# Mixer work entered in steps beside weight pieces, in a hybrid encoder layer on one core

## Chip, cores and metric

The kernel runs on one core of one Trainium2 chip. The metric is the device time of one execution in microseconds (us): 1707.37 for the kernel before, the median of 3 runs (1707.24 to 1707.54).

## What is computed

One layer of a bidirectional encoder over 16 learned meta tokens and 256 tokens of width 2048, all in float32. RMSNorm is followed by one input projection that feeds four token mixers and their output gates; then a SwiGLU block and a final RMSNorm:

```
n = rms_norm(h)                        # h: 272 x 2048
p = n @ w_in                           # 14 mixer columns of 512, 4 gates of 2048
z_A = rglru(p)       # conv of width 4, gates, scans both ways, GeLU gate
z_B = hyena(p)       # conv of width 3, long filters from a small sine network, FFT convolution
z_C = retention(p)   # rotary q and k, decay, GroupNorm, swish gate
z_D = hgrn2(p)       # state expansion 128, forget gates, RMSNorm, swish gate
h = h + (sum_b sigmoid(gate_b) * (z_b @ w_branch_out[b])) @ w_out
h = h + (silu(m @ w_gate) * (m @ w_up)) @ w_down      # m = rms_norm(h)
out = rms_norm(h)[16:]
```

## The kernel before

Every large matrix comes from memory in weight **pieces** of 128 x 1024 float32, 568 of them in a fixed order (`piece`, line 97). A piece is loaded into `raw` (4 buffers) by SP's queue, rounded to `hi` by ACT (line 112), and the remainder `lo` = raw - hi is taken by DVE (line 113); `hi` and `lo` have 3 buffers each. The first NPOOL = 2 pieces are split by POOL. The activations are split in the same way, and a product takes three matmuls: hi with hi, hi with low part, lo with hi. `piece` puts its instructions WAHEAD = 250 places ahead in priority; the order on each engine is then made by a scheduler that takes ready instructions by priority, so the order of the program is a priority and no more.

The **head** (lines 196 to 283) loads the meta tokens and x, sums the squares (`squares`), rescales both token tiles (`rescale`; t = 0 and t = 1, in quarters of 512 columns, by ACT and DVE in turn), transposes them on PE (line 280) and writes the split norm `nh`, `nl` (lines 281 and 282).

The **mixer stage** works through SCHED (line 54), a string of 32 letters. A to E are chunks of 256 projected columns for one mixer (`mix_chunk`, 4 pieces, 96 matmuls of 256 to 272 columns, lines 312 to 314); E is the second pair of heads of mixer D; G is a chunk of 512 gate columns for one branch (`gate`, 8 pieces of 12 matmuls of 512 columns, `xs_gemm`). Each mixer is a generator: it yields when it wants its next chunk, and gets the accumulators. What a mixer does after a chunk enters the program there, as one block:

```
            wants[m] = mixers[m].send(mix_chunk(wants[m]))
```

The large blocks are the filters of B (`filters`, line 339, called before B's fourth chunk), B's transforms after its sixth chunk, mixer D's seven levels after its fifth (lines 612 to 637: `ex` and `copy_predicated` into `sc`), C's rotary products and heads (`rotate`, lines 733 to 754), and A's gates and scans (lines 792 to 828), which follow A's second chunk of four. `head_out` (line 484) normalises heads into `on` and transposes them (line 512); `put_z` splits a mixer's result into `zh`, `zl`. Accumulators have 4 buffers, two per chunk; small products share 4 others (`ps`).

After the mixer stage `up` (line 868) multiplies z by the branch weights in the order BORDER = (1, 3, 2, 0), that is B, D, C and A last, 2 pieces each for one quarter of the columns, alternating with the gates of the next quarter. The output projection, SwiGLU and the last norm follow; the change doesn't touch them.

ACT's functions come from tables that are loaded when the set changes; `lut` keeps groups of functions in order. `late` and `add_manual_dep` order an instruction behind another on its engine.

Of the kernel before, what the change touches and what calls it, by code (L numbers as in the profile page):

```python
# [17 lines left out]
P = 128  # L18
D = 2048
# [13 lines left out]
NPOOL = 2  # L33
WPAD = 64
WAHEAD = 250
# [18 lines left out]
SCHED = "BBBBBCDDDDCBCDECEECCGEECCAGAAGAG"  # L54
# [5 lines left out]
for _name, _w in (("norm_mix", 16), ("norm_ffn", 16), ("lcw", 16), ("lcb", 4), ("lba", 8), ("lbx", 8), ("lam", 8),  # L60
                  ("hcw", 36), ("hcb", 12), ("hbias", 4), ("lb", 4), ("b1", 1), ("b2", 1), ("dec", 8),
                  ("negt", 2), ("nyq", 1), ("ind", P), ("fill", 48)):
    PCOL[_name] = _n
    _n += _w
# [3 lines left out]
def body(tc, a, out):  # L68
# [17 lines left out]
    nc.sync.dma_start(par, a["par"])  # L86
# [6 lines left out]

    wpos = [0]
    first = []

    def piece(kt, cols, dst=None, skip=0):

        i = wpos[0]
        wpos[0] += 1  # L100
        with tc.high_priority(offset=WAHEAD if i >= 6 else 0):
# [11 lines left out]
            ins = (G if i < NPOOL else V).tensor_tensor(lo, raw, hi.bitcast(F32), op=SUB)  # L113
# [82 lines left out]
    G.dma_start(mlp, a["mlp"])  # L196
# [12 lines left out]

    def sines():  # L210
        p1 = ps("pf1")
        PE.matmul(p1[:64, :T], mlp[:33, 0:64], mlp[:33, 128:], start=True, stop=True)
        f1 = TT("f1", T, rows=64)
        sine(f1, p1[:64, :T], pc("b1", rows=64))
        p2 = ps("pf2")
        PE.matmul(p2[:64, :T], mlp[:, 64:128], f1, start=True, stop=True)
        sine(f2[:64], p2[:64, :T], pc("b2", rows=64))
        G.memset(f2[64:], 0.0)
# [20 lines left out]
    def squares(g, engs):  # L239
        for q, e in enumerate(engs):  # L240
            dump = H("dump", 512)
            x, acc = quarter(g, q), ss[:, g, q:q + 1]
            if e == "A":
                A.activation(dump, x, AF.Square, accum_out=acc)
            else:
                V.scalar_tensor_tensor(dump, x, 1.0, x, op0=MUL, op1=MUL, accum_out=acc)
        r = rs[:, g:g + 1]
        V.tensor_reduce(r, ss[:, g], op=ADD, axis=mybir.AxisListType.X)
        rsqrt(r, r, 1.0 / D)

    def rescale(g, engs):
        for q, e in enumerate(engs):
            x, r = quarter(g, q), rs[:, g:g + 1]
            if e == "A":
                A.activation(x, x, AF.Copy, scale=r)
            else:
                V.tensor_scalar(x, x, r, None, op0=MUL)
# [18 lines left out]
    split(nh[:, :, 0:META], nl[:, :, 0:META], nm.rearrange("p k b t -> p (k b) t"))  # L276
    for k in range(KT):
        pt = ps("ptn")
        for t in range(2):
# [3 lines left out]
                                         op0=MUL, op1=SUB)]  # L283

# [54 lines left out]
    def filters():  # L339
        sines()  # L340
        late(0, A.activation(adec, par[:, PCOL["dec"]:PCOL["dec"] + 8], AF.Abs))
        w3 = S("w3", 1024)
        G.dma_start(w3, a["hy_w3"])

        dec = S("dec", 1024)
        G.dma_start(dec, a["hy_decay"].partition_broadcast(P))
        A.activation(dec, dec, AF.Abs)
        fwd_t = S("fwd_t", 2, NFREQ)
        G.dma_start(fwd_t, a["dft"])
        split(fwd[0], fwd[1], fwd_t)  # L350
        hs = [H(f"hs{t}", W) for t in range(2)]
        hd = [H(f"hd{t}", W) for t in range(2)]
        hb = [H(f"hb{t}", W) for t in range(2)]
        for t in range(2):
# [10 lines left out]
            V.tensor_tensor(hd[t], e[:, 0:512], hb[t], op=SUB)  # L365
        for s in range(4):
# [11 lines left out]
            A.copy(spec[s % 2][:, s // 2], pk)  # L378

# [11 lines left out]
        V.tensor_tensor(wrap[:, :, 16:31], wrap[:, :, 16:31], ew[:, 4:8, 14::-1], op=SUB)  # L391

    def mixer_b():
# [19 lines left out]
        split(*inv, inv_t)  # L413

# [9 lines left out]
        for t in range(3):  # L424
# [6 lines left out]
            else:  # L431
                A.copy(utm, pu)
                V.tensor_sub(utm[32:64], pu[32:64], utm[32:64].bitcast(F32))
        ys = []
        for f in range(2):
# [18 lines left out]
            if f == 0:  # L454
                G.tensor_copy(y[0][0:1], rr[0:1])
                G.tensor_copy(y[1][0:1], ii[0:1])
            for i in range(2):
                split(yp[0][:, i], yp[1][:, i], y[i])
            ys.append(yp)
        prod = S("prod", NW, META, META)  # L460
# [3 lines left out]
        V.tensor_reduce(ycor, prod, op=ADD, axis=mybir.AxisListType.X)  # L464
        for wp in range(2):
# [14 lines left out]
            put_z(1, 2 * wp, 2, z)  # L480
        yield


    def head_out(b, pos, gate, group, h0=0):
# [4 lines left out]
        if group:  # L489
            mv = tiny("mv", 4 * n, 2)  # L490
            for i in range(4 * n):
                bs = tiny("bs", 6)
                V.bn_stats(bs, pos[i // 4][:, i % 4 * P:i % 4 * P + P])
                V.bn_aggr(mv[:, i], bs)
            rsqrt(rs, mv[:, :, 1], 1.0)
# [6 lines left out]
        for m in range(n):  # L502
# [12 lines left out]
            put_z(b, h0 + 2 * m, 2, z)  # L515

    def silu(dst, src):
        n = dst.shape[-1]
        sg = TT("sg", n)
        A.activation(sg, src, AF.Sigmoid)  # L520
        V.tensor_tensor(dst, src, sg, op=MUL)  # L521

# [3 lines left out]
    def mixer_d(hp):  # L526
# [36 lines left out]
        for c in range(2):  # L563
            silu(gt[:, c], acc[c][:, META:])
# [3 lines left out]
        A.activation(bs.rearrange("p (h c) t -> p h (c t)", h=2), ff[:, :, META:], AF.Ln)  # L568
# [608 lines left out]
```

## Time and profile before

| | |
|---|---|
| median of 3 runs | 1707.37 us |
| the profiled execution's own time | 1708.65 us |
| its span in the trace | 1706.9 us |
| mean granted TensorE clock | 0.996 |
| PE busy | 1667.4 us (98%) |
| DVE busy | 954.6 us (56%) |
| ACT busy | 803.8 us (47%) |
| POOL busy | 80.6 us (5%) |

The profile is of one execution; its times count from the first instruction of the span. PE is TensorE's matmuls, PEld its weight loads, DVE is VectorE, ACT ScalarE, POOL GpSimd, SPq the DMA queue of SyncE. A matmul's end is modelled, so PE counts as busy a little longer than it is. A bracket after a row tells how long the engine stood idle before it and what ended that.

### The profile page before, as it was taken

The page shows a single profiled execution, that of the slowest core. Times are in us where ns is not written, and L with a number is a line of the kernel's source. Part 1 is how long each engine was busy: PE and PEld are TensorE (multiplying, and loading weights), DVE is VectorE, ACT ScalarE, POOL GpSimd, SP SyncE. Part 2 cuts the span into 40 slices and gives each one's busy share as a digit, 9 for nine tenths or more (in the row PEclk, how much of TensorE's full clock was granted, in tenths as well). Part 3 has the DMA queues.
Part 4 walks back from the last instruction along what each step waited for, and adds up shares of the span by engine and source line. Part 5 has one row for each costly group of instructions (what it writes and reads, how often), then busy time and mean ns, then how long its engine had stood idle before and what let it go on. Part 6 is the DMA issues. An engine that isn't in the chain of part 4 may idle for free.

```text
span 1706.9 us, 22379 instructions
## 1 busy us (share of the span) xinstructions
PE 1667.4 (98%) x8844; PEld 1437.0 (84%) x8844; DVE 954.6 (56%) x1140; ACT 803.8 (47%) x969; POOL 80.6 (5%) x74
## 2 busy tenths in 40 slices
PE   6999999999999999999999999999999999999997
PEld 5999999989978888888888888888888888888886
DVE  6755895486675445454455545454545444544554
ACT  5544465474574444444445544444444334444443
POOL 2000000001002002010020000000000000000001
PEclk9999999999999999999999999999999999999999
DMA  6546444546356555555666555555555555555554
GB/s 238 184 140 193 144 140 145 181 139 212 111 172 211 188 194 186 196 194 188 197 198 210 197 197 186 192 190 187 191 190 188 194 196 190 194 185 190 193 191 142
DMA packets 87225, 313.81 MB, mean 184 GB/s; under 512 B 9824, under 2 KB 10112, under 8 KB 86992
## 3 DMA queue, kind: packets, MB, share of 16 engines
q1 hardware_dynamic: 84960, 304.42, 54.0%
q0 software_dynamic: 2160, 7.97, 1.5%
q8 instruction: 69, 1.13, 0.3%
q14 instruction: 36, 0.29, 0.1%
HBM read 309.17 MB, written 2.10 MB: 182 GB/s over the span
## 4 chain that ended last, share of the span: by engine, by line
PE 93%; DVE 4%; ACT 2%; issue 1%; DMA 0%; SPq 0%; ACTq 0%
PE acc L135 23%; PE acc L136 23%; PE acc L134 23%; PE mix L312 5%; PE mix L314 5%; PE mix L313 5%; DVE lo L113 1%; PE pth L948 1%; PE last L1006 1%; PE last L1005 1%; PE last L1007 1%; DMA x<-in_x_dram 0%; ACT hi L112 0%; PE pl L635 0%; PE pg L801 0%
## 5 line engine op out<-in xcount | busy, mean ns | idle before, releaser
L113 DVE TENSOR_TENSOR lo<-raw,hi 128x1024 fp32r<-128x1024 f32 x556 | 686.5, 1235 | 668.9 <-ACT hi L112 668.6
L112 ACT CAST hi<-raw 128x1024 fp32r<-128x1024 f32 x556 | 585.0, 1053 | 759.9 <-PE acc L136 620.1
L136 PE MATMUL acc<-hi,n2l 128*128 128x512 f32 x704 | 274.0, 389 | 0.0
L135 PE MATMUL acc<-lo,n2h 128*128 128x512 f32 x704 | 273.9, 389 | 0.0
L312 PE MATMUL mix<-nh,hi 128*128 128x272 f32 (+2 forms) x896 | 255.0, 287 | 3.4 <-DVE cg L521 1.8
L314 PE MATMUL mix<-nh,lo 128*128 128x272 f32 (+2 forms) x896 | 252.8, 287 | 4.3 <-DVE lo L113 4.3
L313 PE MATMUL mix<-nl,hi 128*128 128x272 f32 (+2 forms) x896 | 255.9, 287 | 0.0
L134 PE MATMUL acc<-hi,n2h 128*128 128x512 f32 x704 | 249.4, 390 | 0.0
L135 PE MATMUL acc<-lo,nh 128*128 128x512 f32 x512 | 200.1, 391 | 2.8 <-DVE lo L113 2.8
L136 PE MATMUL acc<-hi,nl 128*128 128x512 f32 x512 | 199.8, 390 | 0.0
L134 PE MATMUL acc<-hi,nh 128*128 128x512 f32 x512 | 181.7, 391 | 0.6 <-ACT hi L112 0.6
L312 PEld LDWEIGHTS mix<-nh,hi 128*128 128x128 f32 x896 | 169.9, 190 | 5.9 <-issue 2.8
L314 PEld LDWEIGHTS mix<-nh,lo 128*128 128x128 f32 x896 | 168.6, 190 | 6.1 <-DVE lo L113 5.2
L313 PEld LDWEIGHTS mix<-nl,hi 128*128 128x128 f32 x896 | 170.2, 190 | 0.7 <-issue 0.2
L136 PEld LDWEIGHTS acc<-hi,n2l 128*128 128x128 f32 x704 | 132.1, 188 | 27.5
L134 PEld LDWEIGHTS acc<-hi,n2h 128*128 128x128 f32 x704 | 132.2, 188 | 27.1
L135 PEld LDWEIGHTS acc<-lo,n2h 128*128 128x128 f32 x704 | 132.2, 188 | 27.1
L136 PE MATMUL acc<-hi,hidl 128*128 128x512 f32 x312 | 121.4, 389 | 0.0
L135 PE MATMUL acc<-lo,hidh 128*128 128x512 f32 x312 | 121.4, 389 | 0.0
L135 PEld LDWEIGHTS acc<-lo,nh 128*128 128x128 f32 x512 | 96.1, 188 | 24.0 <-DVE lo L113 4.5
L134 PEld LDWEIGHTS acc<-hi,nh 128*128 128x128 f32 x512 | 96.0, 188 | 20.9 <-ACT hi L112 1.3
L136 PEld LDWEIGHTS acc<-hi,nl 128*128 128x128 f32 x512 | 96.2, 188 | 19.6
(388 smaller groups left out, 1644.7 us busy)
## 6 DMA issues: line engine op xcount, KB each, us to landing
raw<-in_w_dram SPq DMA_DIRECT2D x568, 512.0 KB, 3.3
x<-in_x_dram SPq DMA_DIRECT2D x4, 512.0 KB, 8.7
h<-in_x_dram SPq DMA_DIRECT2D x8, 256.0 KB, 4.2
out_dram<-h SPq DMA_DIRECT2D x8, 256.0 KB, 3.1
lruw<-in_lruw_dram POOLq DMA_DIRECT2D x2, 512.0 KB, 6.3
dm<-in_decay_dram POOLq DMA_DIRECT2D x4, 256.0 KB, 4.3
nf<-in_norm_final_dram POOLq DMA_DIRECT2D x1, 1024.0 KB, 6.6
rot<-ck POOLq DMA_DIRECT2D x2, 272.0 KB, 6.0
```

What stands on the lines that cost most here:

```text
L112: A.copy(hi, raw)
L113: ins = (G if i < NPOOL else V).tensor_tensor(lo, raw, hi.bitcast(F32), op=SUB)
L134: PE.matmul(acc[t], xh[:, k, s], wh[:, j], start=(i + j == 0), stop=False)
L135: PE.matmul(acc[t], xh[:, k, s], wl[:, j], start=False, stop=False)
L136: PE.matmul(acc[t], xl[:, k, s], wh[:, j], start=False, stop=(i + j == n - 1))
L312: PE.matmul(o, wh[:, j, s], nh[:, k, t0:T], start=(k == 0), stop=False)
L313: PE.matmul(o, wh[:, j, s], nl[:, k, t0:T], start=False, stop=False)
L314: PE.matmul(o, wl[:, j, s], nh[:, k, t0:T], start=False, stop=(k == KT - 1))
L948: PE.transpose(pt[:, j * P:j * P + P], s[:, j * P:j * P + P], ident)
L1005: PE.matmul(acc, xh, wh, start=(k == 0), stop=False)
L1006: PE.matmul(acc, xh, wl, start=False, stop=False)
L1007: PE.matmul(acc, xl, wh, start=False, stop=(k == 2 * n - 1))
```

## The change

Every mixer's block is cut by `yield`s of a negative number, the vector work of the step just entered in us. `beside`, called by each `piece`, adds RATE = 1.6 us of credit (kept at 3.2 at most) and enters steps of the busy mixers, first come first, while credit is positive. `through(m)` enters all that is left of a mixer, before its next chunk, before A's first chunk for all mixers, and at the end of the stage. The filters of B become a mixer of their own, F, begun before B's fourth chunk. SCHED takes a new order. A's GeLUs come ahead of its gates, and A's gates wait for its fourth chunk. In the head the squares of both tiles come first and in a fixed order on ACT and DVE, then one quarter of both tiles is rescaled (t = 0 on ACT, t = 1 on DVE), the others between the transposes; POOL splits its two pieces in quarters of 256 columns; 40 transposes of the identity are added on PE; `par` is loaded in two parts, the second behind x; and `mlp` and `rope` are no longer loaded at the start, but behind the first two pieces. The logarithms of D are ordered behind the last sigmoid of its gate.

```diff
-SCHED = "BBBBBCDDDDCBCDECEECCGEECCAGAAGAG"
+SCHED = "BBBBBBDDDDDCCCCCCEEEEECCGGGAAAAG"
+NWARM = 40
+RATE = 1.6
...
-    nc.sync.dma_start(par, a["par"])
+    nc.sync.dma_start(par[:, :PCOL["norm_ffn"]], a["par"][:, :PCOL["norm_ffn"]])
...
+    mixers, wants, busy, credit = {}, {}, [], [0.0]
+
+    def go(m, acc=None):
+        r = mixers[m].send(acc)
+        if r is not None and r < 0:
+            credit[0] += r
+            if m not in busy:
+                busy.append(m)
+        else:
+            wants[m] = r
+            if m in busy:
+                busy.remove(m)
+
+    def beside():
+        credit[0] = min(credit[0] + RATE, 2 * RATE)
+        while busy and credit[0] > 0:
+            go(busy[0])
+
+    def through(m):
+        while m in busy:
+            go(m)
...
     def piece(kt, cols, dst=None, skip=0):
+        beside()
...
             if i < NPOOL:
-                G.tensor_scalar(hi, raw, 1.0, 0.0, op0=MUL, op1=ADD)
+                for j in range(kt):
+                    ins = G.tensor_scalar(hi[:, j], raw[:, j], 1.0, 0.0, op0=MUL, op1=ADD)
+                    if "G" in last:
+                        after(ins, last["G"])
+                    ins = G.tensor_tensor(lo[:, j], raw[:, j], hi[:, j].bitcast(F32), op=SUB)
+                    last["G"] = ins
             else:
-                A.copy(hi, raw)
+                ins = A.copy(hi, raw)
+                if i in behind:
+                    after(ins, behind[i][0])
...
     mlp = H("mlp", 128 + T, rows=64)
-    G.dma_start(mlp, a["mlp"])
...
+    nc.sync.dma_start(par[:, PCOL["norm_ffn"]:], a["par"][:, PCOL["norm_ffn"]:])
...
-    squares(0, "AVAV")
-    squares(1, "AVAV")
     V.tensor_scalar(xm, xm, rs[:, 2:3], None, op0=MUL)
-    rescale(0, "AVAV")
-    rescale(1, "VAVA")
...
+    pw_ = ps("pwarm")
+    for i in range(NWARM):
+        PE.transpose(pw_[:, i % 4 * P:i % 4 * P + P], ident, ident)
+    for t in range(2):
+        for q, e in enumerate("AVAV"):
+            dump = H("dump", 512)
+            x, acc = quarter(t, q), ss[:, t, q:q + 1]
+            if e == "A":
+                ins = A.activation(dump, x, AF.Square, accum_out=acc)
+            else:
+                ins = V.scalar_tensor_tensor(dump, x, 1.0, x, op0=MUL, op1=MUL, accum_out=acc)
+            after(ins, last[e])
+            last[e] = ins
+    V.tensor_reduce(rs[:, 0:2], ss[:, 0:2], op=ADD, axis=mybir.AxisListType.X)
+    rsqrt(rs[:, 0:2], rs[:, 0:2], 1.0 / D)
+    def rescale(q):
+        for t in range(2):
+            x, r = quarter(t, q), rs[:, t:t + 1]
+            if t == 0:
+                ins = A.activation(x, x, AF.Copy, scale=r)
+            else:
+                ins = V.tensor_scalar(x, x, r, None, op0=MUL)
+            after(ins, last["AV"[t]])
+            last["AV"[t]] = ins
+    rescale(0)
     for k in range(KT):
...
+        for e, ins in zip("AV", anchor):
+            after(ins, last[e])
+            last[e] = ins
+        if k % 4 == 1:
+            if k < 12:
+                rescale(k // 4 + 1)
+            behind[NPOOL + k // 4 - 1] = anchor
...
     def mixer_b():
...
-                with tc.issue_after(first[0]):
-                    filters()
+                go("F")
...
+        yield -0.01
+        through("F")
...
     def mixer_d(hp):
...
             V.copy_predicated(sc, masks[:, li][:, None, :].to_broadcast([P, 4, P]),
                               pl.rearrange("p (c n) -> p c n", c=4))
+            yield -3.4
...
     def mixer_a():
...
+        zs = []
+        for wp in range(2):
+            acc = yield META
+            z = H("za", 2, SEQ)
+            for c in range(2):
+                lut(z[:, c], acc[c][:, META:], AF.Gelu_apprx_tanh, new=(wp == c == 0))
+            zs.append(z)
+        yield -0.01
...
             V.tensor_tensor(g, g, xc[:, :, t0:], op=MUL)
+            yield -1.3
...
-    mixers = {"A": mixer_a(), "B": mixer_b(), "C": mixer_c(), "D": mixer_d(0), "E": mixer_d(1)}
-    wants = {}
+    mixers.update({"A": mixer_a(), "B": mixer_b(), "C": mixer_c(), "D": mixer_d(0), "E": mixer_d(1), "F": filters()})
...
+            if m not in wants and m == "A":
+                for x in mixers:
+                    through(x)
             if m not in wants:
-                wants[m] = next(mixers[m])
-            wants[m] = mixers[m].send(mix_chunk(wants[m]))
+                go(m)
+            through(m)
+            go(m, mix_chunk(wants[m]))
+    for m in mixers:
+        through(m)
```

The steps credited, in us: F 2.4, 2.4, 1.2, 2.6 twice, 1.2, 0.1, 1.2, 0.1; B 0.01, 1.2, 0.7 three times, 3.9 and 1.2 twice, 2.0, 2.2 twice; D and E 0.01, 3.6, 0.4, 3.4 seven times, 4.0, 0.1, 2.4; C 3.6, 3.8, 0.1 three times, 0.01, 1.0 four times, 1.6 and 2.4 twice; A 0.01, 1.3, 3.0 and 3.8 twice, 1.2 three times.

## Rows read from the trace of the kernel before

**Rows 1.** The page, busy time, share of the span and instructions of each engine.

```profile
PE 1667.4 (98%) x8844; PEld 1437.0 (84%) x8844; DVE 954.6 (56%) x1140; ACT 803.8 (47%) x969; POOL 80.6 (5%) x74
```

**Rows 2.** Stretches: length; busy us (count) of PE, PEld, DVE, ACT, POOL; PE's clock; DMA.

```profile
220.00:260.00 40.00, 37.46 (x312) 36.77 (x312) 40.00 (x81) 24.73 (x33) 1.03 (x2) 1.00 0.45 141
260.00:300.00 40.00, 36.81 (x283) 36.00 (x282) 18.71 (x28) 20.70 (x34) 0.11 (x1) 0.91 0.46 142
360.00:400.00 40.00, 36.23 (x302) 35.50 (x301) 36.43 (x75) 27.79 (x36) 3.77 (x7) 1.00 0.53 179
440.00:500.00 60.00, 54.91 (x332) 47.39 (x332) 48.35 (x96) 45.21 (x71) 0.00 (x0) 1.00 0.42 137
600.00:1600.00 1000.00, 1000.00 (x4485) 829.34 (x4484) 509.53 (x471) 433.70 (x467) 31.81 (x18) 1.00 0.58 193
```

**Rows 3.** PE's waits: who for whom, us in total, times, longest.

```profile
PE mix L314 <- DVE lo L113: 4.3, 4, 1.5
...
PE acc L135 <- DVE lo L113: 2.8, 4, 1.5
...
PE pt L512 <- DVE on L509: 1.9, 1, 1.9
```

**Rows 4.** Timeline of DVE in mixer D's levels: start, us, engine, line.

```profile
226.04 1.22 DVE L113 TENSOR_TENSOR lo<-raw,hi 128x1024 fp32r<-128x1024 f32 x1
227.18 0.42 DVE L624 TENSOR_TENSOR ex<-pe 128x256 f32<-128x256 f32 x1
227.51 0.42 DVE L621 TENSOR_TENSOR ex<-pe 128x256 f32<-128x256 f32 x1
...
228.52 0.69 DVE L627 TENSOR_TENSOR ex<-ex,q 128x512 f32<-128x512 f32 x1
229.12 0.42 DVE L630 TENSOR_TENSOR ex<-ex,kf 128x256 f32<-128x256 f32 x1
...
237.85 0.74 DVE L636 COPY_PREDICATED sc<-masks,pl 128x512 f32<-128x512 uint8 x1
```

**Rows 5.** Timeline of PE at the same place.

```profile
227.31 0.52 PE L314 MATMUL mix<-nh,lo 128*128 128x272 f32 x2 [0.87 <-DVE lo L113]
```

**Rows 6.** Timeline of the head.

```profile
2.62 0.30 POOL masks.py:199 TENSOR_SCALAR_AFFINE_SELECT ident<-ident 128x128 f32<-128x128 f32 x1
...
12.52 0.88 DVE L257 TENSOR_SCALAR x<-x,rs 128x512 f32<-128x512 f32 x2
...
15.60 2.34 POOL L113 TENSOR_TENSOR lo<-raw,hi 128x1024 fp32r<-128x1024 f32 x1
15.73 0.16 DVE L163 RECIPROCAL rs<-rs 128x1 f32<-128x1 f32 x1 [0.27 <-ACT rs L162]
...
15.93 3.48 DVE L257 TENSOR_SCALAR x<-x,rs 128x512 f32<-128x512 f32 x2
...
18.28 1.12 PE L280 MATMUL ptn<-ident,x 128*128 128x128 f32 x4 [3.87 <-DVE x L257]
...
19.41 0.79 PE L312 MATMUL mix<-nh,hi 128*128 128x272 f32 x2
...
22.22 0.43 PE L314 MATMUL mix<-nh,lo 128*128 128x272 f32 x1
...
22.44 0.43 PE L312 MATMUL mix<-nh,hi 128*128 128x272 f32 x1
...
24.28 0.28 PE L313 MATMUL mix<-nl,hi 128*128 128x272 f32 x1
...
24.40 0.29 PE L314 MATMUL mix<-nh,lo 128*128 128x272 f32 x1
```

**Rows 7.** The tile x: time from a load's issue to its landing.

```profile
DMA to landing us min/median/max: 7.0/8.7/9.8
```

**Rows 8.** Timeline of mixer A: first sigmoid on ACT, first `zl` on DVE.

```profile
450.61 0.49 ACT L144 ACTIVATE r<-pg,par 128x272 f32<-128x272 f32 x1
...
493.98 0.69 DVE L157 TENSOR_TENSOR zl<-za,zh 128x512 fp32r<-128x512 f32 x1
```

More of the change, by code (lines that the diff above doesn't have):

```diff
@@ L92, in body, with after @@
     make_identity(nc, ident)
+    last = {}
+    behind = {}
+    def after(ins, prev):
+        tc.add_manual_dep(ins.ins, prev.ins.name, mybir.DependencyInfo(
+            mybir.DependencyClass.NoSync, mybir.DependencyReason.DATA), reason="order at the head")
+    mixers, wants, busy, credit = {}, {}, [], [0.0]
[16 more added lines that the diff above has]
+            go(m)
     wpos = [0]
@@ L208, in sine @@
         A.activation(dst, x, AF.Sin)
[L210 to L218, printed above, removed]
     warm = tiny("warm", 1)
@@ L339, in filters @@
     def filters():
[L340 to L346, printed above, removed]
+        with tc.issue_after(first[0]):
+            G.dma_start(mlp, a["mlp"])
+            late(0, A.activation(adec, par[:, PCOL["dec"]:PCOL["dec"] + 8], AF.Abs))
+            w3 = S("w3", 1024)
+            G.dma_start(w3, a["hy_w3"])
+            dec = S("dec", 1024)
+            G.dma_start(dec, a["hy_decay"].partition_broadcast(P))
+            fwd_t = S("fwd_t", 2, NFREQ)
+            G.dma_start(fwd_t, a["dft"])
+        p1 = ps("pf1")
+        PE.matmul(p1[:64, :T], mlp[:33, 0:64], mlp[:33, 128:], start=True, stop=True)
+        f1 = TT("f1", T, rows=64)
+        sine(f1, p1[:64, :T], pc("b1", rows=64))
+        yield -2.4
+        p2 = ps("pf2")
+        PE.matmul(p2[:64, :T], mlp[:, 64:128], f1, start=True, stop=True)
+        sine(f2[:64], p2[:64, :T], pc("b2", rows=64))
+        G.memset(f2[64:], 0.0)
+        yield -2.4
         A.activation(dec, dec, AF.Abs)
-        fwd_t = S("fwd_t", 2, NFREQ)
-        G.dma_start(fwd_t, a["dft"])
         split(fwd[0], fwd[1], fwd_t)
+        yield -1.2
         hs = [H(f"hs{t}", W) for t in range(2)]
@@ L365, in filters @@
             V.tensor_tensor(hd[t], e[:, 0:512], hb[t], op=SUB)
+            yield -2.6
         for s in range(4):
@@ L391, in filters @@
         V.tensor_tensor(wrap[:, :, 16:31], wrap[:, :, 16:31], ew[:, 4:8, 14::-1], op=SUB)
+        yield
     def mixer_b():
@@ L413, in mixer_b @@
         split(*inv, inv_t)
+        yield -1.2
         fwd_m = H("fwd_m", NFREQ)
@@ L433, in mixer_b @@
                 V.tensor_sub(utm[32:64], pu[32:64], utm[32:64].bitcast(F32))
+            yield -0.7
         ys = []
@@ L456, in mixer_b @@
                 G.tensor_copy(y[1][0:1], ii[0:1])
+            yield -3.9
             for i in range(2):
@@ L459, in mixer_b @@
             ys.append(yp)
+            yield -1.2
         prod = S("prod", NW, META, META)
@@ L464, in mixer_b @@
         V.tensor_reduce(ycor, prod, op=ADD, axis=mybir.AxisListType.X)
+        yield -2.0
         for wp in range(2):
@@ L480, in mixer_b @@
             put_z(1, 2 * wp, 2, z)
+            yield -2.2
         yield
@@ L494, in head_out @@
                 V.bn_aggr(mv[:, i], bs)
+                if i % 4 == 3:
+                    yield -1.6
             rsqrt(rs, mv[:, :, 1], 1.0)
@@ L515, in head_out @@
             put_z(b, h0 + 2 * m, 2, z)
+            yield -2.4
     def silu(dst, src):
@@ L587, in mixer_d @@
         kfs = kf[:, :, META:]
+        yield -3.6
         vt = H("vt", 2, 2 * P)
@@ L612, in mixer_d @@
         A.copy(sc.rearrange("p c n -> p (c n)"), psd)
+        yield -0.4
         for li, m in enumerate(LEVELS):
@@ L681, in mixer_d @@
                 PE.matmul(o, sm[:, i], vtm[:, c * P:c * P + P], start=False, stop=True)
-        head_out(3, [po], gt, False, 2 * hp)
+        yield -0.1
+        yield from head_out(3, [po], gt, False, 2 * hp)
         yield
@@ L687, in mixer_c @@
         rope = H("rope", 2, T)
-        G.dma_start(rope, a["rope"])
+        with tc.issue_after(first[0]):
+            G.dma_start(rope, a["rope"])
         def rotate(x, n):
@@ L705, in mixer_c @@
         rotate(cq, SEQ)
+        yield -3.6
         ck = S("ck", NW, T)
@@ L711, in mixer_c @@
         rotate(ck, T)
+        yield -3.8
         cv = S("cv", NW, T)
@@ L723, in mixer_c @@
             A.copy(dst, pv)
+            yield -0.1
         cg = S("cg", NW, SEQ)
@@ L728, in mixer_c @@
                 silu(cg[:, 2 * hp + c], acc[c][:, META:])
+        yield -0.01
         pos = []
@@ L745, in mixer_c @@
                 V.tensor_tensor(dmm, pcm[:, 0:SEQ], dmm, op=MUL)
+                yield -1.0
                 for t in range(2):
@@ L753, in mixer_c @@
             pos.append(po)
-        head_out(2, pos, cg, True)
+        yield from head_out(2, pos, cg, True)
         yield
```

55 lines of the change are left out of this document (23 added, 32 removed).

## The prediction

> **What bounds the kernel now.** I read the page's busy times first: TensorE (PE) is at work for 98% of the span and carries the chain, VectorE (DVE) 56%, ScalarE (ACT) 47% [rows 1]. So a gain can only come from time in which PE stands still or runs slowly. The table by stretches says where that is: from 600 to 1600 us nothing at all is lost, and in the mixer stage four stretches lose 2.5, 3.2, 3.8 and 5.1 us, 14.6 in all (length less PE busy) [rows 2]. The stretch from 260 has a granted clock of 0.91 over 40 us besides, some 3.6 us of full speed. The list of PE's waits names the causes: mostly `lo` of a weight piece (DVE, line 113) comes late, or a head output `on` does [rows 3]. One such wait in detail: the `lo` that PE needs starts on DVE at 226.04 behind a run of `ex` subtractions of mixer D, and PE's next matmul starts at 227.31 after 0.87 idle [rows 4, 5]. In that stretch DVE is busy for all of its 40 us. The page counts a matmul as busy to its modelled end, 0.28 to 0.29 us, though one starts each 0.12 [rows 6], so every wait hides 0.16 more; with the 9 waits of rows 3 that is 1.4. The mixer stage thus loses 14.6 + 3.6 + 1.4 = 19.6 us: 14 before 400 us and 5.6 from 440 on. The rest is the head: first mixer matmul at 19.41, at half clock (1.2 of 2.4 GHz) until about 24.2 [rows 6].
>
> **The head.** Today the second token tile's rescales wait: `rs` is ready at 15.89, but the two DVE rescales take 3.48 us together, against 0.88 for two at 12.52, because POOL's 2.34 us `lo` of a weight piece runs beside them [rows 6]. PE's transposes follow at 18.28, the first mixer matmul 1.13 later. After the change the squares of both tiles come first (the first tile's rescales, 0.88 on DVE, no longer stand ahead), one quarter is rescaled before the transposes start, and POOL's work is cut into quarters of some 0.6. So `rs` at 15.0, rescale 0.5 plus up to 0.6 of waiting, transposes to first matmul 1.1: 16.6 to 17.2, and 2.5 us gained. `par` in two parts and `mlp` and `rope` issued later leave the x loads lighter company; they land 7.0 to 9.8 us after issue now [rows 7], so the most that this could give is the spread, 2.8, the least nothing; I take 0.7, nearer the least, since x is by far the largest transfer itself. The later loads are wanted only by the fourth B chunk and by C, tens of us on; if that cover were gone, a transfer would cost its landing time, like the x loads' 7 to 10. Clock: between 19.41 and 24.28 matmuls start each 0.22, later each 0.12 [rows 6]; at full clock this stretch would be 2.1 us shorter. The 40 added transposes keep PE at work ahead of it. They cost 0.28 each at half clock (four in 1.12), 11.2 in all; begun when the identity is made, at 2.92 [rows 6], they end before the 15.5 at which PE is wanted, so I price them at nothing; placed behind the meta token's transposes they could end up to 2 late. Of the 2.1 I take 1.3, since after them PE idles until x is ready. **Head: 2.5 + 0.7 + 1.3 = 4.5 us less**, between 1 and 7.
>
> What that row also bears on: POOL holds up DVE. The Trainium skill, SBUF — State Buffer, section "Who interferes with whom", says that DVE and GpSimd lock one port pair for a whole instruction, also for DVE instructions with two SBUF inputs, and that issue order decides who blocks. That speaks against cutting POOL's work into 16 short instructions: each DVE square or rescale could meet one. By it the four rescales of the second tile would wait 0.6 each, 2.4 in all, and the sum below would be 2.4 higher. The row shows one hold of 2.3 instead; that only the first rescale stands on the path is why I keep 4.5.
>
> **The steps.** Today a mixer's whole block enters the program after its last chunk; now it enters in steps, at most 1.6 us of credit per weight piece. The `yield`s credit F 13.8, B 19.9, D and E 34.3 each, C 19.7, A 19.8: 142 us, 89 of the stage's 144 pieces. Does that fit? In the full stretch DVE's instructions start closer than they last: `lo` 1.14 apart (226.04 to 227.18), a 256-wide one 0.33, a 512-wide one 0.60 [rows 4]. A level of D is six of the second kind, one of the third and a copy of 0.74: 3.3, against 3.4 credited. A piece with steps thus asks 1.14 + 1.6 x 3.3/3.4 = 2.7 of DVE, and gives 24 x 0.123 = 2.95 in a mixer chunk, 12 x 0.223 (1000 us over 4485 starts [rows 2]) = 2.7 in a gate. It just fits, with `lo` never behind more than one step. Unshown is how many waits survive: all 14 us (a bound of no gain) or none. I take 2, nearer none, as a full DVE from 220 to 260 lost only 2.5 in 40. When `lo` is no longer late, the next late thing is a chunk's own evacuation, which PE notices after two chunks. **14 - 2 = 12 us less.** The order on D's logarithms lies on ACT, which is half idle; the loads that F and C now issue stand on POOL behind its 16 short instructions, and POOL is busy 5% [rows 1]. Both cost nothing while that cover stands; without it a late logarithm would hold up one chunk's `hi`.
>
> **The new order.** It puts all of A last: four chunks, one gate, then `up`. A's chain from its first sigmoid to the first `zl` took 450.61 to 494.67, 44 us [rows 8]. It may now start only when the fourth A chunk ends, as the gelus come ahead of its sigmoids. Until `up` wants A's z (fourth in BORDER) PE has one gate, 8 pieces, and three branches of 2: 14 x 2.7 = 38. A's z is 6 us late, unless PE takes the next gate's matmuls first, for which one of three weight buffers is free. So of the 5.6 us lost from 440 on I let 4 come back here: **1.6 less**, between +4 and -5.6.
>
> **Sum.** 4.5 + 12 + 1.6 = 18 us off the profiled execution's own 1708.65, 1690.6. The median of the three runs shown is 1.3 under that execution, so 1689. Differences under 0.2% (3.4 us) are what a measurement of this kernel can't tell from none.
>
> **Rivals.** (1) Everything fits and A's z comes in time: head 6, all 19.6 regained, 1682; with small waits that the 0.16 hides entirely, down to 1675. For it: DVE's mean is 56%. Against: the 44 us chain. Chance 0.2. (2) A's chain is later still and PE's clock falls in that pause, as it did in the stretch with 0.91: 6 + 3.6 in place of 4: 1695, up to 1702. Chance 0.1. (3) The change doesn't do what it says: program order is only a priority for the scheduler, which placed `ex` subtractions of several levels in one run ahead of `lo` [rows 4] though `lo` has priority; if it gathers the steps again, the mixers lose what they do now and only the head gains: 1703, half of it within 0.2%. Chance 0.1. (4) Slower: DVE becomes the bound. If an instruction costs its duration and not its distance (0.42 for 0.33, 0.69 for 0.60, 1.22 for 1.14), a level is 3.95 and a piece with steps wants 1.22 + 1.6 x 3.95/3.4 = 3.08, which is 0.13 over a mixer piece and 0.4 over a gate's; over 89 pieces 12 to 36 us in place of the 19.6: 1695 to 1719, with gates the larger part 1711. It decides from 2.7 us of DVE per piece on. Against it: starts 0.33 apart in the full stretch. Chance 0.1.
>
> **How the numbers follow.** Forecast 0.5 (1682 to 1697), the rivals 0.2, 0.1, 0.1 and 0.1. Faster: 0.5 + 0.2 + 0.1, half of (3), little of (4): 0.84; same 0.07, slower 0.09. From 1675 to 1704 only (4) and half of (3) are left out.
>
> **What would show it.** Right: first mixer matmul near 16 and starts 0.12 apart from the first on; second-tile rescales without holds over 0.6; no PE wait on `lo` or `on` before A; granted clock 1.00 from 260 to 300. A wait of PE for `zl` or `zh` of A in `up`, 4 us, shows the order's price; none refutes it. Wrong: DVE full through C's and the gates' chunks with PE waiting for `lo` at each piece (4), or runs of `ex` instructions of several levels as now (3).

## The result, and the profile after

The changed kernel takes **1694.21 us**, median of 4 runs (1693.87 to 1695.46), beside 1707.30 for the kernel before on the same chip: a ratio of 0.9925, 95% interval 0.9908 to 0.9942. The forecast was 1689, in a range of 1675 to 1704. The profiled execution took 1694.32 with a span of 1692.6, so the profile speaks for the median.

The page's busy times first [rows 1]:

```profile
PE 1668.4 (99%) x8884; PEld 1438.5 (85%) x8884; DVE 957.2 (57%) x1137; ACT 795.7 (47%) x963; POOL 81.9 (5%) x86
```

Every engine does what it did before; only the span is shorter. Where it is shorter shows in the starts of four matmuls and the end of the span, read from the two timelines (us from the start of the span; the differences are worked out from them):

| | before | after | change, in all | change, this part |
|---|---|---|---|---|
| first matmul of a mixer chunk | 19.41 | 15.64 | -3.8 | -3.8 |
| last matmul of the fourth chunk | 73.23 | 69.45 | -3.8 | 0.0 |
| first matmul with z in `up` | 527.22 | 505.63 | -21.6 | -17.8 |
| the same, second quarter of `up` | 636.95 | 622.26 | -14.7 | **+6.9** |
| end of the span | 1706.87 | 1692.55 | -14.3 | +0.4 |

So the head gained 3.8, the mixer stage 17.8, and 6.9 were given back in the first quarter of `up`, whose code the change doesn't touch. The table by stretches shows the same [rows 2]: length, busy us (count) of PE, PEld, DVE, ACT and POOL, PE's clock, DMA.

```profile
220.00:260.00 40.00, 40.00 (x332) 40.00 (x331) 24.96 (x31) 17.31 (x25) 1.12 (x3) 1.00 0.54 173
260.00:300.00 40.00, 40.00 (x344) 40.00 (x343) 22.19 (x28) 21.12 (x32) 0.00 (x0) 1.00 0.51 172
300.00:360.00 60.00, 59.17 (x456) 55.98 (x456) 49.98 (x93) 40.57 (x52) 2.76 (x5) 1.00 0.52 171
360.00:400.00 40.00, 40.00 (x204) 34.07 (x203) 21.53 (x29) 22.79 (x33) 3.25 (x6) 1.00 0.64 213
...
440.00:500.00 60.00, 60.00 (x414) 55.92 (x413) 34.74 (x54) 37.99 (x57) 0.00 (x0) 1.00 0.50 167
500.00:560.00 60.00, 54.80 (x236) 42.58 (x235) 48.78 (x54) 32.52 (x41) 10.91 (x7) 1.00 0.55 184
```

The four stretches that lost 2.5 to 5.1 us each lose nothing now, and the clock of 0.91 from 260 on is 1.00. The order of the chunks is another, so the same stretch isn't the same work: DVE, full from 220 to 260 before, is busy for 24.96 of 40 there, but it is full from 180 to 200 (20.00 of 20 us) and from 330 to 360 (30.00 of 30), where the levels of D and E now run, and PE loses only 0.9 and 0.8 in them. The main loss has moved to 500 to 560. The kernel before had that stretch for nothing, with 14 us less of DVE in it, since A's gates and scans then lay between 450 and 494:

```profile
500.00:560.00 60.00, 60.00 (x293) 50.64 (x292) 34.72 (x34) 28.75 (x31) 11.15 (x7) 1.00 0.64 213
```

PE's waits after the change (who for whom, us in total, times, longest) name what is left [rows 3]:

```profile
PE acc L179 <- DVE lo L155: 4.0, 5, 1.3
...
PE mix L366 <- DVE lo L155: 1.2, 2, 0.9
...
PE acc L180 <- DVE zl L201: 1.0, 1, 1.0
PE acc L178 <- ACT hi L152: 0.6, 1, 0.6
```

The waits for `on` and most of those of the mixers' matmuls are gone. What is left is `lo` ahead of `acc` matmuls, 4.0, nearly all of it between 502 and 528, and then a single wait of 1.0 for A's `zl`. The timeline of DVE there (start, us, engine, line):

```profile
504.90 2.36 DVE L155 TENSOR_TENSOR lo<-raw,hi 128x1024 fp32r<-128x1024 f32 x2
508.27 2.43 DVE L923 TENSOR_TENSOR gi<-gi,r 128x1088 f32<-128x1088 f32 x2 [1.01 <-ACT r L188]
510.62 2.57 DVE L926 TENSOR_TENSOR_SCAN gi<-aa,gi 128x272 f32<-128x272 f32 x4
513.10 1.20 DVE L155 TENSOR_TENSOR lo<-raw,hi 128x1024 fp32r<-128x1024 f32 x1
514.22 2.43 DVE L926 TENSOR_TENSOR_SCAN gi<-aa,gi 128x256 f32<-128x256 f32 x4
...
523.48 3.19 DVE L933 TENSOR_TENSOR za<-za,gi 128x512 f32<-128x512 f32 x2
```

and of ACT and PE at the same place:

```profile
505.83 1.28 ACT L188 ACT_TABLE_LOAD   x1
507.13 2.06 ACT L188 ACTIVATE r<-r 128x1088 f32<-128x1088 f32 x2
509.21 1.28 ACT L188 ACT_TABLE_LOAD   x1
...
511.00 1.04 ACT L152 CAST hi<-raw 128x1024 fp32r<-128x1024 f32 x1
```

```profile
514.36 0.50 PE L179 MATMUL acc<-lo,zh 128*128 128x512 f32 x1 [1.26 <-DVE lo L155]
```

PE wants a `lo` every 2.7 us or so. Between the `lo` pair that ends at 507.26 and the next at 513.10 DVE multiplies A's gates and runs four scans, and ACT spends 505.83 to 511.00 on two table loads, A's square roots and a sigmoid, with no `hi` between them. The chain that ended last (start, us, what) runs through the same work on to `zl`, and from there into PE:

```profile
523.56 3.11 DVE za L933 x2
...
528.86 0.69 DVE zl L201
529.60 0.73 PE acc L180 x2
```

Up to 529.60 PE had lost 6.6 us from 502 on (the distances between its starts beyond the usual 0.227, summed), so without those waits it would have wanted `zl` at about 523, while the `za` that `zl` is made of is begun at 523.48. By this estimate A's z is some 6 us late, and the waits for `lo` ahead of it hide that.

The head (before: [rows 6]), `rs` to the first mixer matmul:

```profile
13.57 0.17 DVE L207 RECIPROCAL rs<-rs 128x2 f32<-128x2 f32 x1 [0.27 <-ACT rs L206]
...
13.77 0.57 DVE L317 TENSOR_SCALAR x<-x,rs 128x512 f32<-128x512 f32 x1
...
14.55 1.18 PE L325 MATMUL ptn<-ident,x 128*128 128x128 f32 x8 [2.69 <-ACT x L315]
...
15.64 0.79 PE L364 MATMUL mix<-nh,hi 128*128 128x272 f32 x2
...
16.32 0.48 DVE L317 TENSOR_SCALAR x<-x,rs 128x512 f32<-128x512 f32 x1
```

The tile x lands a little sooner than before (there 7.0/8.7/9.8 [rows 7]):

```profile
DMA to landing us min/median/max: 4.6/7.8/9.0
```

### The profile page after: what moved, and what is told of

Read it like the earlier page. It is cut to its first block, busy times and chain, and to the rows that moved or that the text cites. A ratio compares the mean times of both kernels' runs of the same rounds, so it can differ in the third digit from the quotient of the medians.

```text
span 1692.6 us, 22467 instructions
## 1 busy us (share of the span) xinstructions
PE 1668.4 (99%) x8884; PEld 1438.5 (85%) x8884; DVE 957.2 (57%) x1137; ACT 795.7 (47%) x963; POOL 81.9 (5%) x86
## 4 chain that ended last, share of the span: by engine, by line
PE 92%; DVE 4%; ACT 2%; DMA 1%; issue 1%; SPq 0%; ACTq 0%; DVEq 0%
PE acc L180 23%; PE acc L179 23%; PE acc L178 23%; PE mix L364 6%; PE mix L366 6%; PE mix L365 6%; DVE lo L155 1%; DMA raw<-in_w_dram 1%; PE pth L1054 1%; DMA x<-in_x_dram 1%; ACT hi L152 0%; PE pl L716 0%; PE pg L899 0%; PE pk L389 0%; DVE held L155 0%
```

## The experiments

Eleven kernels were run, in three groups; the kernel before ran beside each group and took 1707.78, 1708.31 and 1708.28 us (1707.30 beside the changed kernel). Each ratio is to the runs beside it, so kernels of different groups are compared by ratio. The old order of chunks together with the steps wasn't run, so what the order is worth to the steps isn't known.

| label | what | median us | ratio | 95% interval |
|---|---|---|---|---|
| e1_all_at_once | no metering | 1708.43 | 1.0002 | 0.9994 to 1.0011 |
| e4_head_alone | only the head | 1697.70 | 0.9940 | 0.9926 to 0.9953 |
| e6_old_head | all but the head | 1694.97 | 0.9924 | 0.9912 to 0.9937 |
| e5_no_warm | no added transposes | 1695.76 | 0.9926 | 0.9913 to 0.9938 |
| e8_rate_24 | credit 2.4 per piece | 1692.85 | 0.9910 | 0.9895 to 0.9925 |
| e3_a_earlier | A one gate earlier | 1692.24 | 0.9907 | 0.9894 to 0.9921 |
| e7_no_sqrt | A without its roots | 1694.46 | 0.9917 | 0.9903 to 0.9930 |
| e9_no_scan | A without its scans | 1689.30 | 0.9889 | 0.9875 to 0.9902 |
| e11_fine_a | e3 and finer steps in A | 1692.64 | 0.9910 | 0.9896 to 0.9923 |
| e12_a_first | A ahead of all gates | 1694.70 | 0.9921 | 0.9908 to 0.9935 |
| e10_a_earlier_24 | e3 and credit 2.4 | 1695.36 | 0.9923 | 0.9909 to 0.9936 |

### Is it the metering? (e1)

```diff
-RATE = 1.6
+RATE = 1e6
```

All steps of a mixer enter with the next piece, as one block; order and head are the new ones.

> The changed kernel with unlimited credit: each mixer's block enters the program whole at the next piece, as before; order of chunks, A's new order and the head stay as changed. Theory (the metering keeps lo in time): the waits of before come back, 14 to 20 us more than the changed kernel's 1694, so 1706 to 1714, with PE waiting for lo in the stretches after D's and E's last chunks. Rival (the new order of chunks does it, the metering nothing): 1692 to 1697. In between, the gain is shared.

1708.43 us, ratio 1.0002, as the theory had it. Against the changed kernel the metering is worth 14.2 us (1708.43 less 1694.21; 13 by the two ratios), near the 12 that the prediction gave it. Of these, 13.0 lie ahead of the first matmul with z in `up` (518.60 against 505.63). The new order with blocks is worse than the old one: the head alone gives 1697.70 (e4, below), this kernel, with the same head, 10.7 more. In the mixer stage the two differ little (e4 has its first matmul with z at 517.52); most of the 10.7 is lost in the first quarter of `up`, as in the changed kernel. Its waits:

```profile
PE acc L178 <- DVE cg L597: 4.5, 1, 4.5
...
PE acc L179 <- DVE lo L155: 3.6, 4, 1.3
```

The longest on the timeline of PE and, ahead of it, of ACT: the sigmoid `sg` that frees mixer E's chunk starts only at 345.84, behind two `ex` exponentials of other levels and a table load, and the product `cg` with it then stands on DVE behind two `lo`, until 348.34.

```profile
348.93 0.76 PE L178 MATMUL acc<-hi,nh 128*128 128x512 f32 x1 [4.46 <-DVE cg L597]
```

```profile
342.52 2.00 ACT L706 ACTIVATE ex<-ex 128x1024 f32<-128x1024 f32 x2
...
345.84 0.38 ACT L596 ACTIVATE sg<-mix 128x256 f32<-128x256 f32 x1
```

That matmul starts at half clock (0.43 between starts in place of 0.227), and the granted clock of the stretch from 400 to 440 is 0.91 (half from 417.2 to 424.0, behind two waits for a head output `on`). So here blocks cost twice, once in the wait and once in the clock after it.

### Does the size of a step's credit matter? (e8)

```diff
-RATE = 1.6
+RATE = 2.4
```

> The changed kernel with 2.4 us of credit per piece in place of 1.6. Theory (metering keeps DVE's runs between two lo short, and the more a piece may bring the longer they are): between the 1694 of 1.6 and the 1708 of no limit, 1696 to 1703, with waits for lo in the stretches of D's and E's levels. Rival (any metering does, since lo has its place by priority): 1693 to 1695.

1692.85 us, 0.9910, just under what its rival had: half as much again of vector work beside each piece is not slower. DVE is full here too from 180 to 200 and from 330 to 360, yet PE loses 1.3 behind 200 and next to nothing from 320 to 360 (39.97 of 40 busy); `up` loses the same 6.9. So a full DVE over 20 to 30 us doesn't make it the bound of the mixer chunks, and the rival in which it becomes that falls. With e1 it says that the work must be spread out; between 1.6 and 2.4 us per piece no difference can be measured.

### The head alone, and all but the head (e4, e6, e5)

e4 is the kernel before with the head of the changed one (order of squares and rescales, POOL's quarters, the added transposes, `par` in two parts, the later loads); e6 is the changed kernel with the head of before; e5 leaves out the transposes. First e4 against the kernel before, cut to its core, with e6 the other way round against the changed kernel; then e5:

```diff
+NWARM = 40
...
-    squares(0, "AVAV")
-    squares(1, "AVAV")
...
-    rescale(0, "AVAV")
-    rescale(1, "VAVA")
...
+    for i in range(NWARM):
+        PE.transpose(pw_[:, i % 4 * P:i % 4 * P + P], ident, ident)
...
+    rescale(0)
```

```diff
-NWARM = 40
+NWARM = 0
```

> The kernel before with the changed head alone (squares first, quarters, POOL in quarters, 40 transposes, par in two parts, mlp and rope later). Theory (the head gives 3 to 4 us and nothing later takes it back): 1703 to 1704.5. Rival (the mixers' waits fall otherwise and take it back): 1706 to 1708.

> The changed kernel with the head of before. Theory (head and mixers add up): the changed kernel plus 3 to 4 us, 1697 to 1698.5. Rival (the head's gain is lost again in the mixer stage): 1693.5 to 1695.5.

> The changed kernel without the 40 transposes of the identity. Theory (the head goes at the pace at which nh and POOL's quarters come, not at PE's clock): 0 to 1 us more than the changed kernel, 1694 to 1695. Rival (the clock gives 1.3 to 2.1, as in the prediction): 1695.5 to 1697. The granted clock will be half until some us after the first transposes of x in both cases.

The head alone gives 0.9940, some 10 us, more than either of its expectations; all but the head gives 0.9924, 12.8, as its rival had it; both together 0.9925, 13.1. **They don't add.** In e4 the last matmul of the fourth chunk starts at 68.26 against 73.23, so 5.0 of the ten are the head's own (3.8 in the changed kernel, where the last part of x landed 9.0 after its issue, in e4 8.1). Another 5.7 come 200 us later, at a head output of mixer D, whose code is the same in both; 0.9 is lost again by the end of the stage, where e4 has 3.4 us of half clock from 475.6 on. The kernel before waits at that head output twice on PE and runs at half clock from 276.6 to 283.4:

```profile
276.14 1.25 PE L512 MATMUL pt<-ident,on 128*128 128x128 f32 x4 [1.85 <-DVE on L509]
278.73 0.59 PE L312 MATMUL mix<-nh,hi 128*128 128x272 f32 x1 [1.34 <-ACT fb L551]
```

e4 at the same step:

```profile
266.94 0.33 PE L550 MATMUL pt<-ident,on 128*128 128x128 f32 x1 [0.18 <-DVE on L547]
```

ACT's instructions stand in another order there (table loads and `hi` casts around `rsh`); the scheduler chose it anew, presumably since what is ready when had moved by a few us. In the changed kernel that loss is gone with either head, and the head's own gain is partly given back: e6 has its first mixer matmul 3.4 us after the changed kernel and reaches `up` at 508.27, 2.6 after it, and loses 1.6 less in its first quarter (115.0 us from the first matmul with z to that of the second quarter, against 116.6).

e5 is 0.9926 against 0.9925: the 40 transposes are worth nothing that can be measured. Its 1695.76 us lie in the range that its rival had, but the kernel before took 1.0 more beside it than beside the changed kernel, and its profiled execution has 3.4 us of half clock from 529.9 on, some 1.7 us that have nothing to do with the head. Its timeline of PE settles it:

```profile
14.65 1.97 PE L325 MATMUL ptn<-ident,x 128*128 128x128 f32 x8 [8.33 <-ACT x L315]
16.27 0.80 PE L364 MATMUL mix<-nh,hi 128*128 128x272 f32 x2
...
18.23 0.28 PE L366 MATMUL mix<-nh,lo 128*128 128x272 f32 x1
```

Without the transposes PE idles 8.33 us, starts at half clock (0.43 for a matmul of this form), and has full clock (0.28) by 18.23. With them the changed kernel isn't better off: the granted clock is full from 8.6 on, PE idles 2.69 us after them, and the clock is half from 15.4 to 18.8. The comparison that counts is with e3, where PE idled 1.49 and the clock stayed full: from 16.5 on the starts are 0.13 apart. Yet the first matmul of the second chunk starts at 32.74 in e5, at 33.26 in the changed kernel and at 33.16 in e3. The first chunk takes 16.5 us in e5 and 17.6 in the changed kernel, the second 11.8: in the first, PE waits for `nh`, `nl` and POOL's quarters, at either clock.

### Where do the 6.9 us go? (e3, e7, e9)

The prediction had PE waiting in `up` for A's z, which would come late, and the chain above agrees. But if z were all, a z in time would cost nothing. The rivals are ACT's run of table loads and roots without a `hi`, and A's vector work on DVE ahead of `lo`. The kernel before already speaks for a loss that belongs to A's chain: there the same four scans stood ahead of a `lo`, and PE waited for it in the mixer stage.

```profile
481.78 2.57 DVE L826 TENSOR_TENSOR_SCAN gi<-aa,gi 128x272 f32<-128x272 f32 x4
```

```profile
485.51 0.50 PE L135 MATMUL acc<-lo,nh 128*128 128x512 f32 x1 [1.47 <-DVE lo L113]
```

The starts of PE around A's chain lost 4.3 us there (five late starts from 473.97 to 488.98) and 4.1 in the changed kernel (503.21 to 518.42). Of these 4.1, 3.4 stand behind the first matmul with z: so about half of the 6.9 us was lost before the change as well and has only moved. Another 2.6 are new, at 527.86 and 529.60; the rest is spread thinly.

```diff
-SCHED = "BBBBBBDDDDDCCCCCCEEEEECCGGGAAAAG"
+SCHED = "BBBBBBDDDDDCCCCCCEEEEECCGGAAAAGG"
```

> The changed kernel with one gate moved from ahead of A's four chunks to behind them, so that A's chain has 21.8 us more before up wants its z. Theory (the 7 us lost between 500 and 540 are A's late chain): the loss there goes, 1686 to 1689, less what E's and C's remaining steps cost when they enter at once before A (0 to 3). Rival (the loss is up's own load on DVE, beside POOL's additions): the loss stays, 1693 to 1696.

1692.24 us, 0.9907, between its two ranges. With A one gate earlier its z is in time, and from the first matmul with z to that of the second quarter `up` takes 109.8 us, as in the kernel before (109.7). But the stage ahead of it is 4.7 us longer (first matmul with z at 510.37). The stretches show 3.1 of it, 60.00 less 56.90; some 1.5 more are spread over A's own mixer chunks, and what makes them isn't shown:

```profile
440.00:500.00 60.00, 56.90 (x307) 47.94 (x306) 39.25 (x59) 41.71 (x63) 0.00 (x0) 1.00 0.43 148
500.00:560.00 60.00, 60.00 (x270) 49.71 (x269) 36.70 (x37) 27.32 (x30) 11.16 (x7) 1.00 0.63 218
```

with the same wait, between 470 and 520:

```profile
PE acc L179 <- DVE lo L155: 2.5, 3, 1.5
```

So there are two limits, close to each other: with z in time, 4.7 of the 6.9 us are lost all the same, 3 or more of them to late pieces, and that loss goes where A's chain goes.

```diff
-        for d in range(2):
-            lut(rr[d], rr[d], AF.Sqrt, new=(d == 0))
```

```diff
-            for w in range(NW):
-                o = (slice(None), w, slice(None, None, -1 if d else 1))
-                V.tensor_tensor_scan(g[o], aa[o], g[o], 0.0, op0=MUL, op1=ADD)
```

e7 leaves out mixer A's two square roots, e9 its eight scans.

> The changed kernel with A's two square roots left out (the gates are used without the root). Theory (the loss of 7 us from 500 to 540 begins with ACT's unbroken run of table load, two roots, table load and sigmoid, 5.2 us without a hi): the run falls to 2 us and most of the loss goes, 1688 to 1690. Rival (DVE's scans hold up lo): less than 2 gained, 1692 to 1694.

> The changed kernel with A's eight scans left out (5 us of DVE). Theory (ACT's run begins the loss): at most 2.5 gained, 1691.5 to 1694. Rival (DVE's scans hold up lo): 4 to 7 gained, 1687 to 1690.

Without the roots (2.06 us of ACT and their table load) the time is 1694.46; the ratio is 0.0008 lower, the span 0.2 us shorter, neither of which is more than the intervals leave open. The wait for `hi` at 512 is gone, but PE still waits 1.4 for a `lo` and 1.0 for `zl` near 527, and its clock is at half for 3.4 us from 528 on (0.97 over the stretch), which takes back about 1.7; so the roots may be worth 2 us without it, not the whole; of the four executions the one with the highest granted clock (0.999) took 1692.45. Without the scans (5.0 us of DVE) the time is 1689.30 and the span 4.7 us shorter; the ratio, 0.9889, says 6, with 1 to 11 left open by the two intervals. There is no wait for `zl` any more, and from the first matmul with z to that of the second quarter it is 112.1 us. The stretch from 500 in e9:

```profile
500.00:560.00 60.00, 58.55 (x255) 46.55 (x254) 46.05 (x49) 34.97 (x43) 11.51 (x7) 1.00 0.56 198
```

So DVE time taken out of A's chain comes back nearly one for one in the span, as the rival had it. It shortens the chain to z and lets `lo` through, both; the run doesn't part the two, e3 does.

### Its grain, or its amount? (e11, e12, e10)

```diff
-            yield -3.0
+                yield -0.75
...
-            V.tensor_tensor(g, g, rr[d], op=MUL)
             for w in range(NW):
                 o = (slice(None), w, slice(None, None, -1 if d else 1))
+                V.tensor_tensor(g[:, w], g[:, w], rr[d][:, w], op=MUL)
                 V.tensor_tensor_scan(g[o], aa[o], g[o], 0.0, op0=MUL, op1=ADD)
-            yield -3.8
+                yield -0.95
```

> Mixer A one gate earlier, RATE 1.6, and A's squares and scans entered one wide row at a time: a step of 0.75 for each square pair and one of 0.95 for each product and scan, in place of steps of 3.0 and 3.8. Theory: lo of a weight piece is late because A's steps put four scans (2.5 us) on DVE in one run; with the finer steps the 4 to 5 us of waits for lo between 475 and 500 fall to 1 or 2, first matmul of up at 507, 1689 us, ratio 0.989. Rival: it is the amount of A's vector work beside gate pieces, not its grain; the waits stay at 4 or more and the time at 1692, ratio 0.9907.

1692.64 us, span 1690.0, as e3 and as its rival had it. The timeline of DVE says why: although the program enters product and scan of one row at a time, the products stand together, and so do the scans.

```profile
487.15 1.50 DVE L925 TENSOR_TENSOR gi<-gi,r 128x272 f32<-128x272 f32 x4 [1.02 <-ACT r L188]
488.56 0.72 DVE L926 TENSOR_TENSOR_SCAN gi<-aa,gi 128x272 f32<-128x272 f32 x1
489.20 1.41 DVE L925 TENSOR_TENSOR gi<-gi,r 128x256 f32<-128x256 f32 x4
490.52 1.94 DVE L926 TENSOR_TENSOR_SCAN gi<-aa,gi 128x272 f32<-128x272 f32 x3
```

Only after them, at 492.39, comes a `lo`. Here the scheduler gathers, and the program's order doesn't hold; so the run doesn't tell grain from amount on the engine. It does say that the cure isn't in finer yields. Nor did the coarser ones change this chain: its four scans in a run, a `lo` and four more stand on DVE in the changed kernel as they did before.

```diff
-SCHED = "BBBBBBDDDDDCCCCCCEEEEECCGGGAAAAG"
+SCHED = "BBBBBBDDDDDCCCCCCEEEEECCAAAAGGGG"
```

> All four A chunks ahead of all four gates, RATE 1.6. Theory (amount of DVE work beside gate pieces): wherever A's chain stands it costs the same 4 to 5 us, now near 440 to 480, and the time is that of A one gate earlier, 1692 us, ratio 0.9907, up undisturbed at 120.6 us. Rival (A's chain is late for what follows it): with four gates behind it nothing waits, the stage ends 4 us sooner than with the earlier A (first matmul of up at 506), 1688 us, ratio 0.9885. Third: A's chain now meets what mixer E leaves to do on DVE, and the loss grows to 7 or more: 1694.

1694.70 us, 0.9921. `up` is undisturbed (109.7 by the count used above; the expectation's 120.6 goes to a matmul 10.9 later), and the loss stands at 440 to 500, 4.4 us, with a clock of 0.97 besides:

```profile
440.00:500.00 60.00, 55.59 (x235) 44.52 (x234) 40.94 (x52) 36.82 (x50) 0.54 (x1) 0.97 0.53 184
```

Of its three expectations the first holds in kind: the chain costs its 4 to 5 us with two gates behind it or with four. The time is 2.7 over what that expectation had and is the third's: PE loses 2.4 in three places between 378 and 413 (waits for A's own `xc` and `za`, and for a head output `on`), 6.8 in all, and is at half clock for 3.4 us from 461 on. Whether the 2.4 are what E left to do on DVE, as the third had it, isn't shown.

```diff
-RATE = 1.6
+RATE = 2.4
...
-SCHED = "BBBBBBDDDDDCCCCCCEEEEECCGGGAAAAG"
+SCHED = "BBBBBBDDDDDCCCCCCEEEEECCGGAAAAGG"
```

> Mixer A one gate earlier (as in the earlier run with two gates behind A) and RATE 2.4 together. If each had its own gain (late z in one, mixers that finish sooner in the other), they add: 0.9907 less 0.0015, 0.989 of before, about 1689.5 us, and the stage up to the first matmul of up is some 1 us shorter than with the earlier A alone (510.4). Rival: both gain the same thing, an A that is done sooner; then they don't add, 0.990 to 0.991, 1691 to 1692.5, with the same 4 to 5 us of waits for lo between 475 and 500.

1695.36 us, 0.9923: not the sum of the two, nor the better of them, and outside both expectations. The waits for `lo` near 490 are the same; a new one stands at 419:

```profile
422.23 0.59 PE L364 MATMUL mix<-nh,hi 128*128 128x272 f32 x1 [2.84 <-ACT sig L188]
```

```profile
419.69 0.58 ACT L878 ACTIVATE xc<-mix,par 128x272 f32<-128x272 f32 x1
420.28 1.28 ACT L188 ACT_TABLE_LOAD   x1
421.58 1.09 ACT L188 ACTIVATE sig<-acc 128x512 f32<-128x512 f32 x2
```

The sigmoid that frees a gate's accumulators stands behind a `hi`, mixer A's first `xc` and a table load, and PE runs at half clock from 421.0 to 427.8 for it. One such choice of the scheduler undoes two gains. The best kernel measured with the whole computation is e3, 0.9907; its interval overlaps those of the changed kernel, of e8 and of e11, so nothing here is shown to beat the change.

## Why the prediction was right, and where a term was off

**What bounds the kernel.** Right: PE carried the chain, and the gain came from PE's lost time alone.

**The head, 4.5 forecast, 3.8 found.** The rescale term holds: `rs` is ready at 13.74 against 15.89, the second tile's rescale takes 0.57 and 0.48 with no hold, and transposes to first matmul take 1.09 (1.1 forecast). The first mixer matmul is 3.8 earlier, against 2.5 + 0.7 forecast: `rs` was expected at 15.0. x lands 0.8 to 0.9 sooner at the median and at the last, near the 0.7 taken. The port lock of the Trainium skill (SBUF — State Buffer, "Who interferes with whom"), which would have held each of the four rescales by 0.6, doesn't show in them: the longest is 0.57 beside 0.47 for the shortest. What failed is the **clock term of 1.3**: it is worth nothing (e5), because the first chunk is paced by its inputs, and its sign, starts 0.12 apart from the first on, didn't come: they are 0.22 apart until the clock rises at 18.8. The price of 11.2 for the transposes was high as well: the 40 take 5.75 us in all, so the clock rises while they run. That the head comes out near its 4.5 is luck in part: `rs` earlier than forecast makes up for most of a clock term that isn't there.

**The steps and the stage, 17.6 forecast, 17.8 found.** The prediction had 19.6 us lost in the mixer stage, of which it let 2 remain, 17.6 regained before `up`. Found are 17.8, with 0.9 and 0.8 still lost from 100 to 220 and from 300 to 360, so the sign "no PE wait on `lo`" before A held but for 1.6 us. e1 shows that the metering carries it, 13.0 of them in this stage. The near agreement flatters: between 3 and 4 of the 17.8 are the loss of A's chain, most of which has only moved into `up`. The estimate of DVE's load, a piece with steps that just fits, is borne out where the levels of D and E run: DVE is full from 180 to 200 and from 330 to 360, and PE loses little.

**The new order, 4 given back forecast, 6.9 found.** This is the term of the sum that was mis-sized. "A's z is 6 us late" is what the chain shows, but by luck: from A's first sigmoid PE has some 45 us of other work (478.38 to about 523, by the estimate above), not 38, since A's own 32 gate matmuls (`pg`, 6.3 us between 475.6 and 494.2) weren't counted, and the chain takes 50.5, not 44. With the chain of before, z would have been about in time. The discount failed too, "unless PE takes the next gate's matmuls first", by which 4 of 6 were let come back. PE takes none of that time back: 5 to 6 us of it are spent in waits for `hi` and `lo` ahead of z, and 1.0 for `zl` itself, so the sign that was named, a wait of 4 for `zl` or `zh`, is there with 1.0 alone. A's chain from its first sigmoid (478.38) to its first `zl` (528.86) takes 50.5 us instead of 44 [rows 8]; `up`'s own products (`mg`, `sig`) now stand between its parts on DVE, and POOL's additions stretch its last ones. And there is a second cause: where A's chain runs beside pieces of 512 columns, it keeps DVE and ACT from the next `lo`, some 4 us, in the kernel before as in the changed one. The prediction had this among the 5.6 us lost from 440 on and took it as regained by the steps; no run regains it with the whole computation. e3 shows it by itself, 3 us of the 4.7 with z in time; e9 shows that taking 5 us of DVE out of the chain gives about as much back. That no other order would hide it isn't shown: A's chain beside mixer chunks wasn't tried.

**The sum.** Forecast -18.1 on the profiled execution, found -14.3. The 3.8 between them are 2.9 from the order, 0.7 from the head, 0.4 at the end of the span, less 0.2 from the stage.

**The rivals.** The second (1695) has the nearest time, by another way: its longer chain came, but no clock fell (1.00 from 500 to 560). The third, the scheduler gathering the steps, doesn't hold for the blocks of D (e1 against the change) but does in small for A, whose scans stand as before (e11). The fourth, DVE as the bound, falls with e8 for the mixer chunks; for A's chain beside gates something like it is there (DVE busy 18.45 of 20 us from 480 to 500 in e3, PE 16.90), at some 4 us instead of 12 to 36, and it was there before the change.

**One thing that no step of it had:** the parts don't add. Mixers alone are worth 12.8, the head alone 10, both 13.1, because half of what the head gives alone is a loss at 274 us that the changed mixers don't have with either head. So part of what the prediction put down to late `lo` and `on` could be had, by the scheduler's choice, without any metering.

## What to carry to other kernels

When one engine of several feeds the bound one, enter its side work in portions beside each unit of the bound engine's work; that it is spread was worth 13 to 14 us here, and 1.6 or 2.4 us of it per piece made no difference. Count the side work against the tightest stage, not against the mean, and follow a loss to where it goes: the 4 us of one vector-heavy chain went with the chain wherever it was moved, and a stage that looks cured may only have passed it on. And where a scheduler orders the program, measure each part alone and together: an edit of the head changed choices 250 us later, worth as much as the edit itself.

## What the runs showed of the hardware that was not expected

- A half-clock start cost nothing here: the second chunk starts at 32.74 in e5, though PE's matmuls took 0.43 in place of 0.28 until 17.9, and at 33.16 in e3 with a full clock throughout.
- DVE instructions with two inputs in SBUF stretch beside POOL's additions: two `za` products take 3.19 us at 523.48, while POOL adds from 523.12 to 526.12; in e12, where POOL adds nothing then, the same two take 1.29:

```profile
467.63 1.29 DVE L933 TENSOR_TENSOR za<-za,gi 128x512 f32<-128x512 f32 x2
```

  This is the lock of the Trainium skill (SBUF — State Buffer, "Who interferes with whom"): there a DVE instruction with two SBUF inputs contends with a GpSimd instruction that reads SBUF. These traces agree, by 1.9 us for two; it bit in `up`, not in the head's rescales, where the prediction had weighed it.
- Whether half clock follows a wait of PE couldn't be read from the wait. With a wait of 4.5 us PE had half clock for 3.4 us (e1 from 348.9), with one of 2.8 for 6.8 (e10 from 421.0). But e6 has 3.4 us of it from 516.8, behind waits of some 0.8 and 1.5 us, and the changed kernel, with the same two waits before 512.09 and 514.36, has none; e5 has 3.4 us of it from 529.9, behind waits that the changed kernel has as well, at 527.86 and 529.60. Each such 3.4 us cost some 1.7, so a difference of that size between two kernels can be a clock that fell in one of them.
